# A linear-attention layer with one output-gate projection moved ahead of the second value projection, and a bias add and a division taken off VectorE

## The chip, the cores and the metric

One core of one Trainium2 chip runs the whole program. The metric is the device time of one execution in microseconds (us). Three runs of the kernel before gave a median of 1104.21 us (1104.09 to 1104.54).

## The reference, cut to what matters

Two blocks of two layers each work on 256 tokens of width 1024, in float32. The part that matters here is the linear-attention mixer of the second block: 4 heads with keys of width 128 and values of width 256, in chunks of 64 tokens.

```python
q, k, v, g, a_low = split(h @ w_in)
log_a = log_sigmoid(a_low @ w_gate_up + b_gate) / 16
bcum = cumsum(log_a within a chunk);  b_last = last of each chunk
q_in = q * 128 ** -0.5 * exp(bcum);  k_in = k * exp(-bcum);  k_dec = k * exp(b_last - bcum)
o = tril(q_in @ k_in.T) @ v + q_in @ S       # S: state carried over the chunks by k_dec and v
o = o * rsqrt(mean(o * o) + 1e-6) * head_norm_g * silu(g)
x = x + o @ w_out
```

## The kernel before, in words

**Weights.** A list made ahead (`plan_gla`, L1143) gives the order in which weights are loaded and used. Each piece of 128x4x512 float32 (1024 KB) comes by one DMA of SP's queue into one of 4 buffers `raw`, and serves two units of two 128-row blocks. ScalarE rounds a unit to `wh` (L294), VectorE takes the rest `wl = raw - wh` (L312); there are 5 buffers of each, and `unit` (L327) asks for the unit four ahead. Activations are kept as pairs too (`hh`, `hl`), and each product is three matmuls: `wh,hh`, `wl,hh`, `wh,hl` in the profile's names (`mm3`, L358; called a group below).

**Projections.** `proj` (L377) makes 128 tokens x 512 columns in each of two PSUM tiles `up` (3 buffers), for the token halves t = 0 and 1, in 16 groups. `proj_T` (L391) makes the transposed product, with 512 columns per matmul in two tiles; its result goes through `by_row` (L412, L416 and L419). `proj_wide` (L421) makes the first values and the 16 columns `a_low` together.

**Order.** The program is written out in Python. After every group `tick` (L202) advances a count and writes out whatever `after(n, f)` has put into a queue for that count; a consumer whose input isn't written out yet (`Act.wait`, L105) calls `force` (L215) until it is. `self.side` is a generator, `core`, that writes out a step of the attention between groups. A scheduler then puts each engine's instructions in a fixed order; of those whose inputs it takes to be ready, the one written out first goes first.

**The layer.** `gla` (L1151) uses its projections in this order: first values and `a_low` (`proj_wide`), second values (columns 1536), keys (512) and queries (0) by `proj_T`, the gate of heads 0 and 1 (2048), the gate of heads 2 and 3 (2560), then the output projection `accum` (L449) over y blocks 0 to 3 and 4 to 7.

- Five ticks after the first values, `gates` (L1185) turns `a_low` and `gates2` (L1190) makes the decay: a small matmul, the bias on VectorE (L1200, 4 times), `log_sigmoid` for two heads at a time (L900: Exp, Ln and Exp on ScalarE at L906, L910, L911, seven VectorE operations), the division by 16 (L1205, twice), a scan (L1208, 4 times), and the exponentials E, Ei, dec, Ed (L1210 to L1217). Keys and queries are multiplied by these (L1232, L1240).
- `core` (L1261) runs beside the gate projection of heads 0 and 1. Its step for heads 0 and 1 (j = 0) is written out after the 12th of the 16 groups, that of heads 2 and 3 (j = 1) after the 13th. Each makes o in PSUM, sums of squares (L1332, recorded at L556) and `hr` on GpSimd (L561, L563).
- `ev_g` (L1245) takes the gate out of PSUM with Silu (L1248), multiplies by the head gain (L1251, from `row`) and two ticks later calls `fin` (L1337): o times hr times gate (L1342, two per token half), then `prep` (L536): four transposes into the single buffer `tp` (L523), the rounding to `hh` on ScalarE (L509) and the rest `hl` on VectorE (L512). `accum` needs these pairs.

At the start of the program ScalarE is told to load one activation table that serves Exp and Ln (L1540).

Of the kernel before, what the change touches and what calls it, by code (L numbers as in the profile page):

```python
# [11 lines left out]
F32 = mybir.dt.float32  # L12
F32R = mybir.dt.float32r
I32 = mybir.dt.int32
AF = mybir.ActivationFunctionType
ALU = mybir.AluOpType
PSUM = bass.MemoryType.PSUM

P = 128
S = 256  # L20
# [140 lines left out]
class Builder:  # L161
# [981 lines left out]
    def plan_gla(self):  # L1143
        w = self.a["gla_w_in_2"][0]
        self.add_proj(self.a["gla_w_va"], 8, 0, WIDE)
        for c in (1536, 512, 0, 2048, 2560):
            self.add_proj(w, 8, c, 512)
        self.plan_rows(self.a["gla_w_out_2"][0], 0, 4)
        self.plan_rows(self.a["gla_w_out_2"][0], 4, 4)

    def gla(self, h, rs, hook):  # L1151
# [15 lines left out]
        def ev_v(i):  # L1167
            return lambda t, ps: self.scaled(v[t][:, i * 512:(i + 1) * 512], ps, rs[:, t:t + 1])
# [21 lines left out]
        def gates2():  # L1190
            bg = self.vec("bgate")
            z = [self.acc_tile() for _ in range(H)]
            for hd in range(H):
                rows = slice(32 * hd, 32 * hd + 16)
                self.nc.tensor.matmul(z[hd][:, 0:S], wg[rows, 0:P], aT[rows, :], start=True, stop=True,
                                      skip_group_check=True, tile_position=(32 * hd, 0))
            for j in range(2):
                zs = self.tmp_tile()
                for i in range(2):
                    nc.vector.tensor_scalar(out=zs[:, i * S:(i + 1) * S], in0=z[2 * j + i][:, 0:S],  # L1200
                                            scalar1=bg[:, 2 * j + i:2 * j + i + 1], scalar2=None, op0=ALU.add)
                e = [self.tmp_tile() for _ in range(4)]
                o = LA[:, j * 512:(j + 1) * 512]
                self.log_sigmoid(o, zs, e, 512)
                nc.vector.tensor_scalar(out=o, in0=o, scalar1=1.0 / 16.0, scalar2=None, op0=ALU.mult)  # L1205
                for i in range(2):
                    sl = slice((2 * j + i) * S, (2 * j + i + 1) * S)
                    nc.vector.tensor_tensor_scan(out=B[:, sl], data0=self.cst("reset"), data1=LA[:, sl], initial=0.0,  # L1208
                                                 op0=ALU.mult, op1=ALU.add)
            nc.scalar.activation(out=E, in_=B, func=AF.Exp)  # L1210
            nc.scalar.activation(out=Ei, in_=B, func=AF.Exp, scale=-1.0)
            b4 = B.rearrange("p (n c) -> p n c", c=64)
            bl = b4[:, :, 63:64]
            nc.scalar.activation(out=dec, in_=bl.rearrange("p n c -> p (n c)"), func=AF.Exp)
            nc.vector.tensor_tensor(out=Ed.rearrange("p (n c) -> p n c", c=64), in0=bl.to_broadcast([P, 16, 64]),
                                    in1=b4, op=ALU.subtract)
            nc.scalar.activation(out=Ed, in_=Ed, func=AF.Exp)  # L1217

        self.after(DLY[16], gates)
        self.proj(h, 8, 512, ev_v(1))  # L1220
        while self.q:
            self.force()
# [17 lines left out]
                nc.vector.tensor_tensor(out=half(E, b), in0=tk, in1=half(E, b), op=ALU.mult)  # L1240
            self.after(DLY[18], f)

        y = Act(self)

        def ev_g(i):  # L1245
            def f(t, ps):
                gs = self.tmp_tile()
                nc.scalar.activation(out=self.like(gs, ps), in_=ps, func=AF.Silu, scale=rs[:, t:t + 1])  # L1248

                def gain():  # L1250
                    nc.vector.tensor_tensor(out=gs, in0=gs, in1=hg[:, i * 512:(i + 1) * 512], op=ALU.mult)  # L1251
                    self.after(DLY[20], lambda: fin(t, i, gs))

                self.after(DLY[19], gain)
            return f

        oo = {}
        hs = self.small.tile([P, 8], F32, tag="hs", name="hs", bufs=1)
        hr = self.small.tile([P, 8], F32, tag="hr", name="hr", bufs=1)

        def core():  # L1261
            msk = self.gmask_i.unsqueeze(1).to_broadcast([P, H, P])
            kd = []
            both = self.att.tile([P, 2048], F32, tag="bias1", name="both")
            sc = [both[:, t * 1024:t * 1024 + 512] for t in range(2)]
            for s in sc:
                nc.gpsimd.memset(s, 0.0)
            yield 3
            for t in range(2):

                sp = self.up_tile()
                for hd in range(H):
                    for r in (0, 64):
                        sl = slice(hd * S + t * P + r, hd * S + t * P + r + 64)
                        self.mm(sp[r:r + 64, hd * 64:(hd + 1) * 64], Ei[:, sl], E[:, sl], True, True)
                for r in (0, 64):
                    nc.vector.copy_predicated(r4(sc[t])[r:r + 64, :, r:r + 64], msk[r:r + 64, :, r:r + 64],
                                              r4(sp[:, :256])[r:r + 64])
                yield 1
                tp = self.tp_tile()  # L1280
                for hd in range(H):
                    nc.tensor.transpose(tp[:, hd * P:(hd + 1) * P], Ed[:, hd * S + t * P:hd * S + t * P + P], self.ident)
                kk = both[:, t * 1024 + 512:(t + 1) * 1024]
                nc.scalar.copy(kk, tp)
                kd.append(kk)
                yield 1
            S01 = self.att.tile([P, 2048], F32, tag="bias0", name="S01")
            S2 = big("qT1")
            St = [S2 if n == 2 else S01[:, n * 1024:(n + 1) * 1024] for n in range(3)]

            def kv_tiles(j, ns):

                kv = [self.acc_tile() for _ in ns]
                for i in range(2):
                    hd = 2 * j + i
                    for m, n in enumerate(ns):
                        t, r = n // 2, 64 * (n % 2)
                        self.mm(kv[m][:, i * S:(i + 1) * S], kd[t][r:r + 64, hd * P:(hd + 1) * P],
                                v[t][r:r + 64, hd * S:(hd + 1) * S], True, True)
                return kv  # L1300

            def grow(j, n, kv):
                for i in range(2):
                    hd = 2 * j + i
                    sl = slice(hd * S, (hd + 1) * S)
                    nc.vector.scalar_tensor_tensor(out=St[n][:, sl], in0=St[n - 1][:, sl],
                                                   scalar=dec[:, hd * 4 + n:hd * 4 + n + 1],
                                                   in1=kv[:, i * S:(i + 1) * S], op0=ALU.mult, op1=ALU.add)

            for j in range(2):  # L1310
                kv = kv_tiles(j, (0, 1))
                nc.vector.tensor_copy(St[0][:, j * 512:(j + 1) * 512], kv[0])
                grow(j, 1, kv[1])
                yield 1
            for j in range(2):
                grow(j, 2, kv_tiles(j, (2,))[0])
                yield 1
            for j in range(2):
                o = [self.acc_tile() for _ in range(2)]
                heads = range(2 * j, 2 * j + 2)  # L1320
                for t in range(2):
                    for i, hd in enumerate(heads):
                        self.mm(o[t][:, i * S:(i + 1) * S], sc[t][:, hd * P:(hd + 1) * P], v[t][:, hd * S:(hd + 1) * S],
                                i == 0, False)

                for i, n in ((0, 1), (0, 2), (0, 3), (1, 2), (1, 1), (1, 3)):
                    t, r, hd = n // 2, 64 * (n % 2), heads[i]
                    self.mm(o[t][r:r + 64, i * S:(i + 1) * S], E[:, hd * S + n * 64:hd * S + n * 64 + 64],
                            St[n - 1][:, hd * S:(hd + 1) * S], False, True)
                for t in range(2):  # L1330
                    for i in range(2):
                        self.square_sum(hs[:, 4 * j + 2 * t + i:4 * j + 2 * t + i + 1], o[t][:, i * S:(i + 1) * S], S, 1.0 / 16.0)  # L1332
                    oo[t, j] = o[t]
                self.rsqrt(hr[:, 4 * j:4 * j + 4], hs[:, 4 * j:4 * j + 4])
                yield 1

        def fin(t, j, gs):  # L1337
            o = oo.pop((t, j))
            yy = self.tmp_tile()
            for i in range(2):  # L1340
                sl = slice(i * S, (i + 1) * S)
# [6 lines left out]
        while self.q:  # L1348
            self.force()
        self.side = core()  # L1350
        self.proj(h, 8, 512, ev_g(0))
        while self.side is not None:
            self.step()
        self.proj(h, 8, 512, ev_g(1))
        acc = self.new_acc()
        self.accum(acc, y, [0, 1, 2, 3], True, False)
        self.accum(acc, y, [4, 5, 6, 7], False, True, self.add_x(hook))
# [395 lines left out]
```

## Time and profile before

| | |
|---|---|
| median of 3 runs | 1104.21 us |
| the profiled execution's own time | 1104.49 us |
| its span, first to last instruction | 1102.7 us |
| mean granted TensorE clock | 0.997 |
| busy: PE / VectorE (DVE) / ScalarE (ACT) / GpSimd (POOL) | 1087.3 / 801.4 / 609.2 / 30.4 us |

An engine's idle time matters only where it ends up as a wait of the engine that bounds the span. Times in the rows are counted from the span's start; a row's second number is the time from the first start to the last end of the instructions that it merges. DVE and ACT rows overlap slightly at their ends, because the next instruction starts while the one before drains.

### The profile page before, as it was taken

Reading aid. Unit: us, or ns where it says so; the run is one execution under the profiler, and the core shown is the slowest. Engines: PE = TensorE matmul, PEld = TensorE weight load, DVE = VectorE, ACT = ScalarE, POOL = GpSimd, SP = SyncE. Lnnn points to the kernel's source line nnn. Section 1 sums busy time; section 2 is a strip of 40 time slices with the busy share of each in tenths; the row PEclk is TensorE's granted clock in tenths of the full one; section 3 lists DMA queues with packets and bytes.
Section 4 is the critical chain, followed back from the end, with each engine's and each line's share of the span. In section 5 each row is a group of like instructions: output and inputs, shape, how many; then the busy total and the mean of one; then the engine's idle time right before and its main releaser. Section 6 shows DMA issues by size and latency. Waiting matters only on the chain.

```text
span 1102.7 us, 19201 instructions
## 1 busy us (share of the span) xinstructions
PE 1087.3 (99%) x7769; PEld 1003.4 (91%) x7769; DVE 801.4 (73%) x1200; ACT 609.2 (55%) x927; POOL 30.4 (3%) x55
## 2 busy tenths in 40 slices
PE   9999999999999999999999999999999999999997
PEld 7987999999988999999897899999999999999996
DVE  6687756556687766555788578787787768987786
ACT  6466655445665555545664556555555446565563
POOL 1000000000000000000010000000000000000001
PEclk9999999999999999999999999999999999999998
DMA  9844466655563566665555354566665664657551
GB/s 335 298 165 145 162 195 206 210 193 173 142 207 128 172 192 204 206 200 192 194 180 183 108 178 155 179 197 217 201 220 193 197 204 153 189 194 224 188 166 74
DMA packets 137801, 207.30 MB, mean 188 GB/s; under 512 B 10528, under 2 KB 65008, under 8 KB 137712
## 3 DMA queue, kind: packets, MB, share of 16 engines
q1 hardware_dynamic: 136576, 203.89, 56.8%
q10 hardware_dynamic: 1136, 2.17, 0.5%
q8 instruction: 61, 1.00, 0.4%
q14 instruction: 28, 0.23, 0.1%
HBM read 204.97 MB, written 1.07 MB: 187 GB/s over the span
## 4 chain that ended last, share of the span: by engine, by line
PE 87%; DVE 7%; ACT 2%; DMA 1%; issue 1%; SPq 0%; ACTq 0%; DVEq 0%
PE up L339 52%; PE acc L339 33%; DVE wl L312 2%; DMA raw<-fox_w_in 1%; ACT wh L294 1%; PE acc L523 1%; PE tp L523 1%; ACT p L697 1%; DVE p L716 1%; DVE x L602 0%; DVE p L707 0%; PE tp L533 0%; DVE tmp L1365 0%; DVE pT L725 0%; DVE kT L1232 0%
## 5 line engine op out<-in xcount | busy, mean ns | idle before, releaser
L312 DVE TENSOR_TENSOR wl<-raw,wh 128x1024 fp32r<-128x1024 f32 (+2 forms) x373 | 452.3, 1219 | 223.4 <-ACT wh L294 222.4
L294 ACT CAST wh<-raw 128x1024 fp32r<-128x1024 f32 (+2 forms) x373 | 388.8, 1043 | 381.7 <-PE up L339 253.1
L339 PE MATMUL up<-hh,wh 128*128 128x256 f32 x1564 | 431.7, 276 | 0.0
L339 PE MATMUL up<-hh,wl 128*128 128x256 f32 x1564 | 430.1, 275 | 0.0
L339 PE MATMUL up<-hl,wh 128*128 128x256 f32 x1564 | 429.4, 275 | 0.0
L339 PEld LDWEIGHTS up<-hh,wh 128*128 128x128 f32 x1564 | 300.1, 192 | 2.9 <-issue 1.5
L339 PEld LDWEIGHTS up<-hh,wl 128*128 128x128 f32 x1564 | 300.1, 192 | 0.9
L339 PEld LDWEIGHTS up<-hl,wh 128*128 128x128 f32 x1564 | 299.8, 192 | 0.3 <-DVE hl L512 0.2
L339 PE MATMUL acc<-wh,hh 128*128 128x512 f32 (+1 forms) x606 | 227.4, 375 | 0.2 <-DVE mx L716 0.2
L339 PE MATMUL acc<-wh,hl 128*128 128x512 f32 (+1 forms) x606 | 225.1, 371 | 0.1
L339 PE MATMUL acc<-wl,hh 128*128 128x512 f32 (+1 forms) x606 | 224.8, 371 | 0.0
L339 PEld LDWEIGHTS acc<-wh,hl 128*128 128x128 f32 x606 | 114.5, 189 | 15.4 <-DVE hl L1374 0.5
L339 PEld LDWEIGHTS acc<-wh,hh 128*128 128x128 f32 x606 | 114.6, 189 | 15.0 <-DVE mx L716 0.6
L339 PEld LDWEIGHTS acc<-wl,hh 128*128 128x128 f32 x606 | 114.7, 189 | 13.4
L1365 DVE SCALAR_TENSOR_TENSOR tmp<-tmp,vecs,tmp 128x255 f32<-128x255 f32 x192 | 78.0, 479 | 15.2 <-ACT tmp L1363 15.2
L339 PE MATMUL up<-wh,hh 128*128 128x512 f32 (+4 forms) x142 | 52.2, 370 | 1.8 <-DVE tmp L419 1.8
L339 PE MATMUL up<-wl,hh 128*128 128x512 f32 (+4 forms) x142 | 49.9, 352 | 0.2 <-DVE wl L312 0.2
L339 PE MATMUL up<-wh,hl 128*128 128x512 f32 (+4 forms) x142 | 49.8, 353 | 0.1
L1363 ACT ACTIVATE tmp<-tmp,vecs 128x256 f32<-128x256 f32 x96 | 40.9, 496 | 0.0
L1373 ACT CAST hh<-tmp 128x512 fp32r<-128x512 f32 x58 | 34.1, 619 | 8.3 <-DVE tmp L1418 8.3
L1374 DVE TENSOR_TENSOR hl<-tmp,hh 128x512 fp32r<-128x512 f32 x58 | 38.3, 685 | 0.0
L339 PEld LDWEIGHTS up<-wh,hh 128*128 128x128 f32 x142 | 26.8, 189 | 8.1 <-issue 5.5
(205 smaller groups left out, 769.8 us busy)
## 6 DMA issues: line engine op xcount, KB each, us to landing
raw<-ffn_w_up SPq DMA_DIRECT2D x176, 256.0 KB, 4.2
raw<-ffn_w_up SPq DMA_DIRECT2D x32, 1024.0 KB, 5.3
raw<-ffn_w_down SPq DMA_DIRECT2D x32, 1024.0 KB, 5.0
raw<-ffn_w_down SPq DMA_DIRECT2D x44, 512.0 KB, 6.6
raw<-sc_w_in SPq DMA_DIRECT2D x12, 1024.0 KB, 5.3
raw<-fox_w_in SPq DMA_DIRECT2D x10, 1024.0 KB, 9.7
raw<-gla_w_in SPq DMA_DIRECT2D x10, 1024.0 KB, 5.0
raw<-fox_w_out SPq DMA_DIRECT2D x4, 1024.0 KB, 5.2
```

The source lines that it names most:

```text
L294: self.last_hi = nc.scalar.copy(hi[:, :kn, :w], self.raws[r][:, k:k + kn])
L312: self.last_wl = nc.vector.tensor_tensor(out=u.lo[:, :kn, :w], in0=self.raws[r][:, k:k + kn], in1=u.hi[:, :kn, :w].bitcast(F32), op=ALU.su ...
L339: self.nc.tensor.matmul(out, lhsT, rhs, start=start, stop=stop, skip_group_check=True)
L523: self.nc.tensor.transpose(tp[:, i * P:(i + 1) * P], src[:, i * P:(i + 1) * P], self.ident)
L697: self.nc.scalar.activation(out=p[:, o:o + n], in_=p[:, o:o + n], func=AF.Exp, scale=scale, bias=nm[:, j:j + 1], accum_out=sm[:, j:j + 1])
L716: self.nc.vector.tensor_tensor_reduce(out=p[:, o:o + n], in0=lgs[h][:, w], in1=bias(h)[:, w], scale=1.0, scalar=NEG, op0=ALU.add, op1=ALU. ...
L1363: nc.scalar.activation(out=out, in_=z, func=AF.Copy, scale=w[:, 2:3])
L1365: nc.vector.scalar_tensor_tensor(out=out[:, d:], in0=z[:, :S - d], scalar=w[:, 2 - d:3 - d], in1=out[:, d:], op0=ALU.mult, op1=ALU.add)
L1373: nc.scalar.copy(hi, src)
L1374: nc.vector.tensor_tensor(out=lo, in0=src, in1=hi.bitcast(F32), op=ALU.subtract)
```

## The change

- The plan and the calls put the gate projection of heads 0 and 1 (columns 2048) right behind the first values, ahead of the second values. `core` now runs beside the gate projection of heads 2 and 3, which the output projection follows at once.
- The finished gate of heads 0 and 1 waits in two buffers of another pool until `core` has made o; `core` calls `fin` for these heads 4 and 5 ticks after their o. For heads 2 and 3 it is still called two ticks after the gain.
- The bias moves to ScalarE (Identity with a bias read from PSUM). The division by 16 goes: the scan runs over undivided logarithms, and the four exponentials take 1/16 as their scale.

```diff
     def plan_gla(self):
-        for c in (1536, 512, 0, 2048, 2560):
+        for c in (2048, 1536, 512, 0, 2560):
             self.add_proj(w, 8, c, 512)
...
                 for i in range(2):
-                    nc.vector.tensor_scalar(out=zs[:, i * S:(i + 1) * S], in0=z[2 * j + i][:, 0:S],
-                                            scalar1=bg[:, 2 * j + i:2 * j + i + 1], scalar2=None, op0=ALU.add)
+                    nc.scalar.activation(out=zs[:, i * S:(i + 1) * S], in_=z[2 * j + i][:, 0:S], func=AF.Identity,
+                                         bias=bg[:, 2 * j + i:2 * j + i + 1])
...
                 self.log_sigmoid(o, zs, e, 512)
-                nc.vector.tensor_scalar(out=o, in0=o, scalar1=1.0 / 16.0, scalar2=None, op0=ALU.mult)
...
-            nc.scalar.activation(out=E, in_=B, func=AF.Exp)
-            nc.scalar.activation(out=Ei, in_=B, func=AF.Exp, scale=-1.0)
+            nc.scalar.activation(out=E, in_=B, func=AF.Exp, scale=1.0 / 16.0)
+            nc.scalar.activation(out=Ei, in_=B, func=AF.Exp, scale=-1.0 / 16.0)
...
         self.after(DLY[16], gates)
+        y = Act(self)
+        oo, gates_of = {}, {}
+
+        def ev_g(i):
+            def f(t, ps):
+                gs = self.tmp_tile() if i else self.att.tile([P, 768], F32, tag="pT", name=self.name("gs"), bufs=2)[:, :512]
+                nc.scalar.activation(out=self.like(gs, ps), in_=ps, func=AF.Silu, scale=rs[:, t:t + 1])
+
+                def gain():
+                    nc.vector.tensor_tensor(out=gs, in0=gs, in1=hg[:, i * 512:(i + 1) * 512], op=ALU.mult)
+                    gates_of[t, i] = gs
+                    if i:
+                        self.after(DLY[20], lambda: fin(t, i))
+
+                self.after(DLY[19], gain)
+            return f
+
+        self.proj(h, 8, 512, ev_g(0))
         self.proj(h, 8, 512, ev_v(1))
...
                 self.rsqrt(hr[:, 4 * j:4 * j + 4], hs[:, 4 * j:4 * j + 4])
+                if j == 0:
+                    for t in range(2):
+                        self.after(4 + t, lambda t=t: fin(t, 0))
                 yield 1
...
         self.side = core()
-        self.proj(h, 8, 512, ev_g(0))
+        self.proj(h, 8, 512, ev_g(1))
         while self.side is not None:
             self.step()
-        self.proj(h, 8, 512, ev_g(1))
         acc = self.new_acc()
         self.accum(acc, y, [0, 1, 2, 3], True, False)
```

## Rows read from the trace of the kernel before

**Rows 1.** The page: busy time of each engine over the whole span.
```profile
PE 1087.3 (99%) x7769; PEld 1003.4 (91%) x7769; DVE 801.4 (73%) x1200; ACT 609.2 (55%) x927; POOL 30.4 (3%) x55
```

**Rows 2.** Waits of PE over the whole span: total us, times, longest us.
```profile
PE up L339 <- DVE tmp L419: 1.8, 1, 1.8
```

**Rows 3.** The chain that ended last, 585 to 600 us: start, us, what.
```profile
589.85 2.27 DVE wl L312 x2
592.12 0.68 DVE tmp L419 x2
...
592.93 3.99 PE up L339 x28
```

**Rows 4.** Stretches: length, PE, PEld, DVE, ACT, POOL busy (instructions), clock, DMA.
```profile
558.00:593.00 35.00, 33.25 (x253) 30.99 (x253) 33.52 (x50) 22.31 (x31) 0.00 (x0) 1.00 0.55 180
580.00:593.00 13.00, 11.25 (x99) 10.85 (x97) 13.00 (x19) 7.87 (x9) 0.00 (x0) 1.00 0.54 191
```

**Rows 5.** VectorE's groups, 568 to 593 us: busy us, mean ns.
```profile
L312 DVE TENSOR_TENSOR wl<-raw,wh 128x1024 fp32r<-128x1024 f32 x9 | 10.9, 1220 | 0.3 <-ACT wh L294 0.3
...
L1200 DVE TENSOR_SCALAR tmp<-acc,vecs 128x256 f32<-128x256 f32 x2 | 1.0, 480 | 0.0
L1205 DVE TENSOR_SCALAR LB<-LB 128x512 f32<-128x512 f32 x2 | 0.8, 418 | 0.0
```

**Rows 6.** ScalarE in order of time, 557 to 588 us.
```profile
557.46 0.48 ACT L616 ACTIVATE v<-up,rs 128x264 f32<-128x264 f32 x1 [1.89 <-POOL rs L1132]
...
568.74 1.25 ACT L616 ACTIVATE v<-up,rs 128x512 f32<-128x512 f32 x2
...
573.96 0.63 ACT L906 ACTIVATE tmp<-tmp 128x512 f32<-128x512 f32 x1 [1.11 <-DVE tmp L905]
...
587.05 1.06 ACT L1217 ACTIVATE kT<-kT 128x1024 f32<-128x1024 f32 x1
```

**Rows 7.** DMA issues over the span: KB each, us to landing.
```profile
row<-gla_head_norm_g ACTq DMA_DIRECT2D x1, 512.0 KB, 5.4
```

**Rows 8.** PE in order of time around the last steps of the attention.
```profile
616.14 0.48 PE L339 MATMUL up<-wh,hh 128*128 128x512 f32 x1
...
618.19 0.38 PE L339 MATMUL up<-wh,hh 128*128 128x512 f32 x1
...
622.72 0.60 PE L523 MATMUL tp<-ident,tmp 128*128 128x128 f32 x4
...
629.43 0.38 PE L339 MATMUL acc<-wh,hh 128*128 128x512 f32 x1
```

**Rows 9.** GpSimd, the scaling of heads 0 and 1.
```profile
613.73 1.01 POOL L563 TENSOR_TENSOR hr<-hr,mhalf 128x4 f32<-128x4 f32 x1
```

**Rows 10.** ScalarE in order of time, 617 to 624 us.
```profile
617.38 1.28 ACT L1248 ACT_TABLE_LOAD   x1
618.68 0.69 ACT L1248 ACTIVATE tmp<-up,rs 128x512 f32<-128x512 f32 x1
...
619.62 0.69 ACT L1248 ACTIVATE tmp<-up,rs 128x512 f32<-128x512 f32 x1
620.19 2.06 ACT L294 CAST wh<-raw 128x1024 fp32r<-128x1024 f32 x2
623.36 0.58 ACT L509 CAST hh<-tp 128x512 fp32r<-128x512 f32 x1 [1.12 <-PE tp L523]
```

**Rows 11.** VectorE in order of time, 609 to 628 us.
```profile
619.40 0.69 DVE L1251 TENSOR_TENSOR tmp<-tmp,row 128x512 f32<-128x512 f32 x1 [8.88 <-ACT tmp L1248]
620.22 0.48 DVE L1342 SCALAR_TENSOR_TENSOR tmp<-acc,hr,tmp 128x256 f32<-128x256 f32 x1
...
626.79 0.69 DVE L512 TENSOR_TENSOR hl<-tp,hh 128x512 fp32r<-128x512 f32 x1 [0.30 <-ACT hh L509]
```

**Rows 12.** Half-microsecond stretches at the end of the span, columns as in rows 4.
```profile
1094.50:1095.00 0.50, 0.05 (x1) 0.00 (x0) 0.50 (x2) 0.00 (x0) 0.30 (x1) 1.00 0.00 0
...
1096.50:1097.00 0.50, 0.00 (x0) 0.00 (x0) 0.32 (x3) 0.50 (x3) 0.00 (x0) 0.53 0.00 0
```

More of the change, by code (lines that the diff above doesn't have):

```diff
@@ L1209, in gates2 @@
                                                  op0=ALU.mult, op1=ALU.add)
-            nc.scalar.activation(out=E, in_=B, func=AF.Exp)
-            nc.scalar.activation(out=Ei, in_=B, func=AF.Exp, scale=-1.0)
+            nc.scalar.activation(out=E, in_=B, func=AF.Exp, scale=1.0 / 16.0)
+            nc.scalar.activation(out=Ei, in_=B, func=AF.Exp, scale=-1.0 / 16.0)
             b4 = B.rearrange("p (n c) -> p n c", c=64)
             bl = b4[:, :, 63:64]
-            nc.scalar.activation(out=dec, in_=bl.rearrange("p n c -> p (n c)"), func=AF.Exp)
+            nc.scalar.activation(out=dec, in_=bl.rearrange("p n c -> p (n c)"), func=AF.Exp, scale=1.0 / 16.0)
             nc.vector.tensor_tensor(out=Ed.rearrange("p (n c) -> p n c", c=64), in0=bl.to_broadcast([P, 16, 64]),
                                     in1=b4, op=ALU.subtract)
-            nc.scalar.activation(out=Ed, in_=Ed, func=AF.Exp)
+            nc.scalar.activation(out=Ed, in_=Ed, func=AF.Exp, scale=1.0 / 16.0)
         self.after(DLY[16], gates)
+        y = Act(self)
[12 more added lines that the diff above has]
+        self.proj(h, 8, 512, ev_g(0))
         self.proj(h, 8, 512, ev_v(1))
@@ L1241, in ev_q @@
             self.after(DLY[18], f)
[L1243 to L1257, printed above, removed]
         hs = self.small.tile([P, 8], F32, tag="hs", name="hs", bufs=1)
@@ L1334, in core, with fin @@
                 self.rsqrt(hr[:, 4 * j:4 * j + 4], hs[:, 4 * j:4 * j + 4])
+                if j == 0:
+                    for t in range(2):
+                        self.after(4 + t, lambda t=t: fin(t, 0))
                 yield 1
-        def fin(t, j, gs):
-            o = oo.pop((t, j))
+        def fin(t, j):
+            o, gs = oo.pop((t, j)), gates_of.pop((t, j))
             yy = self.tmp_tile()
```

## The prediction, made before the changed kernel was run

> **What bounds the kernel now.** I read the page first: PE is busy for 1087.3 of 1102.7 us [rows 1], so a reordering that adds and removes no matmuls can only win or lose waits of PE, and all of them together are 15.4 us. Next come the waits of PE by releaser. One lies in this layer: 1.8 us, once, for VectorE's L419 [rows 2]. The chain that ended last tells why L419 is late: two `wl` of 2.27 us together run ahead of it, and the chain changes from VectorE to PE only at 592.93 [rows 3]. The wait sits between the query projection and the gate projection behind it: the latter's second PSUM tile is one of the query's, and L419 empties it. The windows then show that this is a backlog and no single late instruction: VectorE is busy 33.52 of the 35 us from 558 to 593, and 13.00 of the last 13.00, while ScalarE has 22.31 of 35 [rows 4]. So the change is aimed at the right engine, and **its prize is at most about 1.8 us**, 0.16% of the run.
>
> Then I looked at where the changed kernel will want data sooner than now. Now a whole gate projection stands between the end of the attention and the output projection: it starts at 618.19, the output projection at 629.43 [rows 8], and the last `hl` that the first four blocks need starts at 626.79 and takes 0.69 [rows 11], 1.9 us early. The change removes this 11 us cover, because its first gate projection has been spent ahead of the values.
>
> **VectorE's relief.** Four bias adds of 0.48 and two divisions of 0.42 leave VectorE [rows 5]: 2.8 us. With the gate projection, four `wl` of 1.22 [rows 5] and two gains (L1251) of 0.69 [rows 11] move into the stretch, 6.3 us, and PE's time for it grows by a projection, some 10.5 us (the 11.2 above less two sets of four transposes). So 33.5 - 2.8 + 6.3 = 37.0 us stand in about 45 where 33.5 stood in 35; the backlog goes, and with it the 1.8 us. What can be late next at that place is one `wl` ahead of L419, 1.2 us; I take nothing for it and keep 0 to 1.2 for the range.
>
> **ScalarE's load.** The bias on ScalarE isn't in the trace. Its nearest row is a scaled copy out of PSUM, 128x264 in 0.48 us [rows 6]; four are 1.9 us. Two Silu of 0.69 come ahead [rows 10]. They will run where the second values are now taken out, at 568.74, between the Exp, Ln and Exp of the first two heads and the next Exp at 573.96 [rows 6]. Silu loads its own table, 1.28 us [rows 10]; the set that serves Exp and Ln together was asked for by hand at L1540 and isn't asked for again. So between one table (a single load back) and three (Exp, Ln, Exp apart) come after it: with Silu's own, 2 to 4 added loads. I take 4, 5.1 us. With four more `wh` of 1.03 (half of the 2.06 for two) [rows 10] ScalarE gets 22.3 + 1.9 + 1.4 + 5.1 + 4.1 = 34.8 of 45 us. Three loads lie in the chain of the decay, which ends now with L1217 at 588.1 [rows 6]; less 2.8 and plus 3.8 it ends near 589, while the keys come out only when the key projection ends, about 10.5 us later than now. Cost on the path: nothing, hidden by the moved projection; without that cover it would be the 1.0 us. Silu also frees PSUM for the second values; their first tile is the third buffer, so groups of the other token half can go first. I keep 0 to 0.5 for this.
>
> Here a rule speaks against the change: "ScalarE: Activation LUTs" of the Trainium skill, in "What ACT_TABLE_LOAD costs", tells to expect about 2.66 us for each change of set, a drain of 1.38 behind the load included. This trace doesn't agree: the load takes 1.28 from 617.38 [rows 10], and Silu starts at 618.68, at once after its end. By the page four changes would be 10.6 us and the decay would end some 4 us later than I have it, still before the attention needs the queries, so the sum would be the same.
>
> **DMA and queues.** SP's queue issues the same pieces of the same size in another order of columns, each when its buffer comes free: no cost. The gain's row goes out on ScalarE's queue ahead of the first values and lands in 5.4 us [rows 7]; the moved gain comes a whole projection later.
>
> **The new wait.** Use the clock of before for the end of the attention, as its steps and the 16 groups beside it are the same. The o of heads 2 and 3 is done when the group at 616.14 begins; three groups of 0.68 end at 618.19 [rows 8]. GpSimd has `hr` for heads 0 and 1 by 614.74 [rows 9], and VectorE idles 8.9 us up to 619.40 [rows 11], so `fin` can run early. Its four transposes can't: they are written out after the last group of the projection, and PE has groups ready until 618.19. From there the path is transposes (0.60 [rows 8]), rounding (0.58 [rows 10]), rest (0.69 [rows 11]): 1.9 us, of which the transposes' 0.4 are work done today as well. That is the lower bound: 1.5 us of wait.
> But ScalarE isn't free. The table load of the second gate starts at 617.38, the Silu of its second token half ends at 620.31, and then a `wh` of 1.03 for the output weights is both ready (its buffer comes free at 618.19) and written out ahead of the rounding [rows 10]. So the rounding runs from about 621.2 to 621.8 and the rest to 622.6: a wait of 4.0 us behind the transposes. On VectorE two `fin` operations of 0.48 [rows 11] for heads 2 and 3 stand ahead of the rest too, which makes up to 5.0. I take 4.5, in the middle, since both are in front by the order of writing. The second token half follows through the single `tp` buffer, but four groups of the first half (2.7 us) cover its 1.9; blocks 4 to 7 have the whole first half of the output projection.
>
> **Sum.** 4.5 - 1.8 = 2.7 us on the profiled execution's own 1104.49 (span 1102.7 and 1.8 around it), or 1107.2. The median of the runs is 0.3 lower than that execution, so I predict **1106.9 us**. About 0.2%, or 2.2 us, is what a measurement of this kernel can tell from no change.
>
> **Rivals.**
> - *In time (0.28).* The transposes get between the last groups, or the rounding gets ahead of Silu and `wh`, so the new wait is 0 to 1.5 us and the 1.8 is won: 1102.4 to 1103.9, not slower. For it: o, `hr` and the gate are all there by 614.74, 3.4 us before the projection ends, and the scheduler does move instructions: half of `fin` (620.22) comes ahead of the second gain, written out earlier [rows 11]. Against it: PE would have to pass over ready groups. It decides at a new wait under 1.8 us.
> - *The clock falls (0.22).* An idle PE can lose its clock: the last matmul ends by 1094.6 and the granted clock reads 1.00 until 1096.5, then 0.5, the lower of the two levels [rows 12]. So 2 us of idleness sufficed there, and 1.8 at 592 did not (clock 1.00 [rows 4]). If a 4.5 us wait does it, each group after it costs 0.68 more until the clock is back. No row shows a return; between nothing and four groups (2.7 us) I take three: 1109.
> - *Nothing is won (0.08).* Table loads and Silu delay the decay or `wl`, and L419 is late as now: 1104.2 + 4.5 = 1108.7. Against it: 8 us of slack on VectorE.
>
> "TensorE: Matmul & The Clock Gate" of the Trainium skill, in "Why this matters for your kernels", likewise warns of idle PE gaps in mid-kernel; the end of this trace agrees.
>
> **How the numbers follow.** The forecast has 0.42; of its 4.0 to 5.0 less 1.8, with up to 0.5 unwon, a quarter stays within 2.2 us. Slower by over 0.2%: 0.32 + 0.21 + 0.06 = 0.59. Within: 0.10 + 0.22 + 0.02 = 0.34. Faster by over 0.2% needs the whole prize and something that I don't see: 0.07. The range runs from the full prize, 1102.4, to the clock's rival with its upper end, 1109.6; alone, the forecast's range is 1106 to 1108.
>
> **What would show it.** Right: no PE wait on L419; a PE wait of 4 to 5 us at the first matmul of the output projection, released by `hl` L512, with Silu and `wh` just ahead of L509 on ScalarE; five table loads in this layer instead of one. Wrong: transposes of heads 0 and 1 between the last groups of the gate projection, and no new PE wait over 1.8 us.

## The result, and the profile after

The changed kernel takes **1110.7 us** (median of 4 runs, 1110.23 to 1111.28), beside 1104.38 (1104.09 to 1104.57) for the kernel before on the same chip: a ratio of 1.0058 [1.0046, 1.0070] (in brackets, here and below, the 95% interval), slower by 6.3 us. Forecast were 1106.9 and, as range, 1102.4 to 1109.6: the sign was right, the loss more than twice the 2.7 forecast, and the time lies above the range. The profiled execution took 1110.23 with a span of 1108.5; before it was 1104.49 and 1102.7.

The page, busy time of each engine, after [rows 1]:

```profile
PE 1090.8 (98%) x7769; PEld 1005.9 (91%) x7769; DVE 799.6 (72%) x1194; ACT 615.5 (56%) x935; POOL 30.4 (3%) x55
```

VectorE has six instructions fewer. ScalarE has eight more, the four biases and four table loads. PE has the same 7769 matmuls but is busy 3.5 us longer: a first sign that some of them ran at a lower clock.

Waits of PE from 585 to 645 us, after: total us, times, longest us [rows 2]:

```profile
PE tp L523 <- DVE tmp L1349: 2.2, 1, 2.2
PE tp L523 <- DVE hl L512: 1.4, 1, 1.4
PE acc L339 <- ACT hh L509: 0.7, 1, 0.7
```

The wait on L419 is gone, which was the prize. In its place stand three new ones, all between the last group of the gate projection of heads 2 and 3 and the second group of the output projection. PE in order of time there [rows 8]:

```profile
626.39 0.38 PE L339 MATMUL up<-wl,hh 128*128 128x512 f32 x1
626.60 0.38 PE L339 MATMUL up<-wh,hl 128*128 128x512 f32 x1
629.17 0.83 PE L523 MATMUL tp<-ident,tmp 128*128 128x128 f32 x4 [2.19 <-DVE tmp L1349]
630.68 0.62 PE L339 MATMUL acc<-wh,hh 128*128 128x512 f32 x1 [0.68 <-ACT hh L509]
...
633.11 1.11 PE L523 MATMUL tp<-ident,tmp 128*128 128x128 f32 x4 [1.38 <-DVE hl L512]
...
634.44 0.63 PE L339 MATMUL acc<-wh,hh 128*128 128x512 f32 x1
634.87 0.64 PE L339 MATMUL acc<-wl,hh 128*128 128x512 f32 x1
```

Compare the distance from start to start: 0.21 us in the first two rows, 0.43 us (634.44 to 634.87) in the last two, for a matmul of the same size. The clock has halved. Windows over this stretch, after (columns as in [rows 4]; the clock is the third number from the end):

```profile
628.00:630.00 2.00, 0.83 (x4) 0.41 (x4) 1.97 (x5) 1.87 (x4) 1.33 (x2) 1.00 0.00 0
630.00:632.00 2.00, 1.05 (x3) 0.33 (x2) 2.00 (x6) 0.59 (x1) 0.00 (x0) 0.72 0.00 0
632.00:634.00 2.00, 0.89 (x5) 0.90 (x5) 2.00 (x4) 0.00 (x0) 0.00 (x0) 0.50 0.00 0
...
636.00:638.00 2.00, 2.00 (x8) 1.61 (x8) 0.00 (x0) 0.01 (x1) 0.00 (x0) 0.57 0.00 0
638.00:640.00 2.00, 2.00 (x12) 1.59 (x11) 0.76 (x2) 1.63 (x2) 0.00 (x0) 1.00 0.00 0
```

From about 630.9 to 637.7 the granted clock is 0.5, that is 1.2 instead of 2.4 GHz, long after PE has work again at 633.11. What holds PE up before that is on VectorE, in order of time [rows 11]:

```profile
628.03 0.69 DVE L1230 TENSOR_TENSOR tmp<-tmp,row 128x512 f32<-128x512 f32 x1 [8.88 <-ACT tmp L1227]
628.63 1.65 DVE L1349 SCALAR_TENSOR_TENSOR tmp<-acc,hr,gs 128x256 f32<-128x256 f32 x4
630.21 0.68 DVE L1230 TENSOR_TENSOR tmp<-tmp,row 128x512 f32<-128x512 f32 x1
630.80 1.65 DVE L1349 SCALAR_TENSOR_TENSOR tmp<-acc,hr,tmp 128x256 f32<-128x256 f32 x4
632.37 0.68 DVE L512 TENSOR_TENSOR hl<-tp,hh 128x512 fp32r<-128x512 f32 x1
```

VectorE stands idle for 8.88 us and then does in one run what PE waits for. The `fin` of heads 0 and 1 (L1349 with `gs`) has had its inputs since 623.4, when GpSimd's `hr` was done, but in VectorE's fixed order it stands behind the gain (L1230) of heads 2 and 3, and that waits for Silu. ScalarE in order of time [rows 10]:

```profile
626.01 1.28 ACT L1227 ACT_TABLE_LOAD   x1
627.31 0.69 ACT L1227 ACTIVATE tmp<-up,rs 128x512 f32<-128x512 f32 x1
...
628.25 0.69 ACT L1227 ACTIVATE tmp<-up,rs 128x512 f32<-128x512 f32 x1
628.82 1.05 ACT L294 CAST wh<-raw 128x1024 fp32r<-128x1024 f32 x1
630.04 0.59 ACT L509 CAST hh<-tp 128x512 fp32r<-128x512 f32 x1 [0.17 <-PE tp L523]
```

**Where the time went.** Two starts on PE serve as anchors: the last matmul of the last gate projection (before 629.21, after 626.60), and the first matmul of the next layer, `up<-hh,wh` (before 652.01, after 658.00). Before:

```profile
629.21 0.38 PE L339 MATMUL up<-wh,hl 128*128 128x512 f32 x1
...
652.01 0.27 PE L339 MATMUL up<-hh,wh 128*128 128x256 f32 x1
```

After, the second one (the first stands above):

```profile
658.00 0.27 PE L339 MATMUL up<-hh,wh 128*128 128x256 f32 x1
```

Up to the first anchor the changed kernel is 2.6 us ahead: 1.8 of L419, and two sets of transposes (0.36 each, 0.72) that it has still to do; the rest is 0.1. Between the anchors it takes 31.40 instead of 22.80 us, 8.6 more, of which 0.72 are those transposes. That leaves 7.9 us for the wait and the clock together; the experiments divide them.

### The profile page after: what moved, and what is told of

It is laid out like the page before. It is cut to its first block, busy times and chain, and to the rows that moved or that the text cites. A ratio compares the mean times of both kernels' runs of the same rounds, so it can differ in the third digit from the quotient of the medians.

```text
span 1108.5 us, 19201 instructions
## 1 busy us (share of the span) xinstructions
PE 1090.8 (98%) x7769; PEld 1005.9 (91%) x7769; DVE 799.6 (72%) x1194; ACT 615.5 (56%) x935; POOL 30.4 (3%) x55
## 3 DMA queue, kind: packets, MB, share of 16 engines
q10 hardware_dynamic: 1136, 2.17, 0.6%
## 4 chain that ended last, share of the span: by engine, by line
PE 88%; DVE 6%; ACT 3%; DMA 1%; issue 1%; SPq 0%; ACTq 0%; DVEq 0%
PE up L339 52%; PE acc L339 34%; DVE wl L312 2%; DMA raw<-fox_w_in 1%; ACT wh L294 1%; PE acc L523 1%; PE tp L523 1%; ACT p L697 1%; DVE p L716 1%; DVE x L602 0%; DVE p L707 0%; PE tp L533 0%; SPq L264 0%; DVE tmp L1371 0%; ACT junk L556 0%
```

## The experiments

Two theories at the start. *The move*: the cover that the gate projection gave to the end of the attention is gone, and all of the loss stands between the two anchors. *Its rival*: table loads, biases on ScalarE or the other order of weights cost something elsewhere. Within the move, the wait's length was claimed by VectorE's order, by ScalarE's queue and by the clock.

**e1: only the relief of VectorE, in the kernel before.**

```diff
-                    nc.vector.tensor_scalar(out=zs[:, i * S:(i + 1) * S], in0=z[2 * j + i][:, 0:S],
-                                            scalar1=bg[:, 2 * j + i:2 * j + i + 1], scalar2=None, op0=ALU.add)
+                    nc.scalar.activation(out=zs[:, i * S:(i + 1) * S], in_=z[2 * j + i][:, 0:S], func=AF.Identity,
+                                         bias=bg[:, 2 * j + i:2 * j + i + 1])
...
-                nc.vector.tensor_scalar(out=o, in0=o, scalar1=1.0 / 16.0, scalar2=None, op0=ALU.mult)
...
-            nc.scalar.activation(out=E, in_=B, func=AF.Exp)
+            nc.scalar.activation(out=E, in_=B, func=AF.Exp, scale=1.0 / 16.0)
```

(and so for the other three exponentials)

> The kernel before with the bias on ScalarE and without the division, all projections in the old order. If the wait of 1.8 us on L419 is VectorE's backlog, 2.8 us less work removes it: no PE wait on L419 and 1102.6 us. If the projection had to move for that, the wait stays and the time is 1104.4.

Measured: 1102.65 us (1102.17 to 1103.00), ratio 0.9985 [0.9976, 0.9994]: 1.6 us faster than before. All that is left of the wait of 1.8 [rows 2] is this (waits of PE, 560 to 640 us):

```profile
PE up L339 <- DVE tmp L419: 0.3, 1, 0.3
```

The anchors stand at 627.84 and 650.64, 22.80 apart as before: everything gained is gained ahead of the first.

**e3 and e8: the division alone, the bias alone.** e3 has the hunks of e1 on the division and the exponentials, e8 the one on the bias.

> The kernel before with the division alone taken away (scales of 1/16 in the exponentials). VectorE loses 0.84 us: if the wait is its backlog, about half of it goes, 1103.3 to 1103.7. If only the order counts, 1104.3.

> The kernel before with the bias alone on ScalarE. VectorE loses 1.9 us of work, a little more than the wait on L419: if its backlog is the whole wait, 1102.6 to 1102.9. If the wait comes from the order of two wl ahead of L419 and not from the backlog, 1104.3.

Measured: 1103.75 (0.9994 [0.9985, 1.0003]) without the division, with 1.2 us left of the wait on L419; 1103.36 (0.9992 [0.9983, 1.0001]) with the bias on ScalarE, with 1.0 left. So 0.84 us of division took 0.6 off the wait, 1.92 us of bias 0.8, and both together, 2.76 us, took 1.5: a microsecond taken off VectorE is worth 0.4 to 0.7 here. The first two biases bring nothing: without them VectorE waits 0.96 us for the same biases on ScalarE (e1 and e8, at L904). The other two take 0.39 each from start to start in VectorE's row before (570.02 to 570.41) and the divisions 0.33 each, together 1.4 us, near the 1.5. Each time by itself is inside what this measurement can tell; but their gains, 0.6 and 1.0, add up to the 1.6 of e1. Both expectations missed a little: e3 lies just above its 1103.3 to 1103.7, and e8 lies between its two values, since it had counted all four biases in full.

**e2: the moved projection without the relief.** The changed kernel with bias and division back on VectorE (the diff of e1, reversed).

> The changed kernel with bias and division put back on VectorE: the moved projection alone. If the loss is all in the new wait behind the last gate projection, and the move itself has slack enough for VectorE, the time is that of the changed kernel, 1110 to 1111, with no wait on L419. If the relief is what removes that wait, it comes back and the time is 1112 to 1113.

Measured: 1111.23 (1110.72 to 1112.16), 1.0066 [1.0052, 1.0079]. Waits of PE, 585 to 645 us:

```profile
PE tp L523 <- DVE tmp L1350: 2.2, 1, 2.2
PE tp L523 <- DVE hl L512: 1.2, 1, 1.2
PE acc L339 <- ACT hh L509: 0.7, 1, 0.7
PE up L339 <- DVE tmp L419: 0.5, 1, 0.5
```

The time lies between the two that were expected. The same three waits and nearly the whole loss come from the move alone; the clock is at 0.50 from 632 to 638 here too. The move by itself takes the wait on L419 from 1.8 to 0.5, and the relief beside it is worth at most the last 0.5 (the ratios of the two kernels overlap). So each half of the change does most of what the other does for L419, and only one of them has a price.

**e4: `fin` of heads 0 and 1 written out earlier.** It is called 1 and 2 ticks after o instead of 4 and 5.

```diff
-                        self.after(4 + t, lambda t=t: fin(t, 0))
+                        self.after(1 + t, lambda t=t: fin(t, 0))
```

> The changed kernel with fin of heads 0 and 1 written out 1 and 2 ticks after their o instead of 4 and 5, its transposes still written out after the projection. If VectorE's fixed order (fin behind the second gate's gain) sets the new wait, the transposes start at once when the projection ends, the wait falls by 2 us or more, the clock stays up and the time is under 1107. If the rounding and the rest behind Silu and the other heads' fin set it, about 1 us is saved and the clock still falls: 1109 to 1110.

Measured: 1110.28 (1109.51 to 1110.99), 1.0053 [1.0040, 1.0065]; only 0.4 under the changed kernel, within the scatter of both, and a little over the 1109 to 1110 expected for this case. VectorE and PE, in order of time:

```profile
623.67 1.66 DVE L1349 SCALAR_TENSOR_TENSOR tmp<-acc,hr,gs 128x256 f32<-128x256 f32 x4 [4.27 <-POOL hr L563]
...
630.16 0.48 DVE L1349 SCALAR_TENSOR_TENSOR tmp<-acc,hr,tmp 128x256 f32<-128x256 f32 x1 [1.18 <-POOL hr L563]
...
631.16 1.26 DVE L1349 SCALAR_TENSOR_TENSOR tmp<-acc,hr,tmp 128x256 f32<-128x256 f32 x3
632.34 0.68 DVE L512 TENSOR_TENSOR hl<-tp,hh 128x512 fp32r<-128x512 f32 x1
```

```profile
627.08 0.60 PE L523 MATMUL tp<-ident,tmp 128*128 128x128 f32 x4
630.67 0.48 PE L339 MATMUL acc<-wh,hh 128*128 128x512 f32 x1 [3.00 <-ACT hh L509]
...
633.07 1.11 PE L523 MATMUL tp<-ident,tmp 128*128 128x128 f32 x4 [1.70 <-DVE hl L512]
```

`fin` is done by 625.3 and the transposes stand right behind the last group, 2.1 us earlier than after, and `hl` still starts at 632.34 (after: 632.37). The first wait has only moved to the next stations: `hh` waits on ScalarE for Silu and a `wh` (629.08 to 630.02), and `hl` on VectorE for the `fin` operations of heads 2 and 3. This is the path on which the prediction counted the wait, with one part that it did not have: the first of those operations waits 1.18 us for GpSimd's `hr` of heads 2 and 3, and the last sum of squares for that runs on ScalarE behind Silu (628.16). What this wait costs by itself no run shows.

The clock falls here too, but later. It is still at 1.00 behind the wait of 3.0 us (window), falls at about 632.7, in the second wait, and is back at 636.1: 3.4 us at half clock, where the changed kernel has 6.8.

```profile
630.00:632.00 2.00, 0.70 (x2) 0.30 (x2) 1.84 (x5) 0.62 (x2) 0.13 (x1) 1.00 0.00 0
```

**e5: e4, with the transposes of heads 0 and 1 written out together with their `fin`.**

```diff
-            self.after(DLY[21], lambda: self.prep(yy, t, list(range(4 * j, 4 * j + 4)), [(y, None)]))
+            self.after(DLY[21] if j else 0, lambda: self.prep(yy, t, list(range(4 * j, 4 * j + 4)), [(y, None)]))
```

> As the run before it, and the transposes of heads 0 and 1 are written out with no delay, so that they stand between the last groups of the gate projection. If the missing cover is the whole loss, no PE wait over 0.5 us is left at the output projection, the clock stays at its upper level, and only the win on L419 remains: 1102.4 to 1103.5. If something else in the new order costs time (table loads, the bias on ScalarE), it stays above 1105.

Measured: 1103.71 (1103.50 to 1104.83), 0.9997 [0.9988, 1.0005], 0.2 over the range expected. PE in order of time:

```profile
623.96 0.83 PE L523 MATMUL tp<-ident,tmp 128*128 128x128 f32 x4 [0.40 <-DVE tmp L1349]
...
627.35 0.60 PE L523 MATMUL tp<-ident,tmp 128*128 128x128 f32 x4
...
628.43 0.38 PE L339 MATMUL up<-wh,hl 128*128 128x512 f32 x1
628.65 0.38 PE L339 MATMUL acc<-wh,hh 128*128 128x512 f32 x1
```

The output projection follows the gate projection 0.22 us later, with no wait; the anchors are 22.93 apart (before 22.80). Two delays in the order of writing, this and e4's, take back 7.0 us. So the loss isn't in the other order of weights, nor in table loads: it is that the last steps of heads 0 and 1 were written out where nothing was left to lie under. Yet e5 is 1.06 us above e1 (its profile has PE waits of 0.4 for `fin` and 0.2 for Silu's tile, where e1 has only the 0.3 on L419), so even without its loss the move has nothing to offer that the relief hasn't given.

**e6: the changed kernel with PE kept busy through the first wait.** It adds work whose result isn't read.

```diff
+        wm = self.up_tile()
+        for i in range(16):
+            nc.tensor.transpose(wm[:, (i % 4) * P:(i % 4 + 1) * P], self.ident, self.ident)
         acc = self.new_acc()
```

> The changed kernel with 16 more transposes of the identity on PE (into a free PSUM tile that nobody reads) between the last group of the gate projection and the transposes of heads 0 and 1. They fill most of the first 2.2 us of the wait and computed nothing is used. If the fallen clock costs 2.5 to 3 us by itself, the clock now stays at its upper level and the time falls to 1107.5 to 1108.5, although PE has more to do. If the wait alone is the loss, the time stays at 1110.7 or rises.

Measured: 1109.77, but from 1108.43 to 1111.05, 1.0050 [1.0037, 1.0062]: the median missed what was expected. The profiled execution, one of the shorter at 1108.7, had the clock at 1.00 in all windows of this stretch, among them this one:

```profile
632.00:634.00 2.00, 0.27 (x2) 0.27 (x3) 2.00 (x5) 0.00 (x0) 0.00 (x0) 1.00 0.00 0
```

Its `hl` starts 5.77 us after the first anchor (633.00 and 627.23), exactly as after (632.37 and 626.60), and its anchors are 29.26 apart instead of 31.40. With the same wait, the clock is thus worth 2.1 us in this execution. Whether the clock fell nevertheless in the longer executions is not shown: there is no trace of one, and their mean granted clock, 0.997 beside 0.998 in the two shortest, differs no more than it does among executions of the kernel before (0.997 to 0.999).

**e7: e4, with the rounding of heads 0 and 1 ahead of `wh`, and `fin` of heads 2 and 3 four ticks later.**

```diff
-                        self.after(DLY[20], lambda: fin(t, i))
+                        self.after(DLY[20] + 4, lambda: fin(t, i))
...
+        y.wait(0, 0)
         acc = self.new_acc()
```

> As the run with fin written out early, and further: the rounding and rest of the first token half are written out ahead of the next weights, and fin of heads 2 and 3 four ticks later. If the queues of ScalarE and VectorE set the length of the wait, the rest (hl) comes about 1.2 us earlier (two fin operations and one wh less ahead of it) and the time falls by 1 to 2 us, to 1108.5 to 1109.3. If the transposes behind the last group set it, nothing changes: 1110.3.

Measured: 1109.05 (1108.64 to 1109.77), 1.0044 [1.0031, 1.0058], with waits of 2.0 for `hh` and 1.0 for `hl` where e4 has 3.0 and 1.7. The queues of ScalarE and VectorE do set the wait's length, but the clock still falls, at about 629.4, right behind the first wait of 2.0 us (windows):

```profile
628.00:630.00 2.00, 0.71 (x2) 0.44 (x2) 0.82 (x2) 2.00 (x5) 1.33 (x2) 0.85 0.00 0
630.00:632.00 2.00, 0.99 (x5) 0.54 (x4) 2.00 (x5) 0.18 (x1) 0.00 (x0) 0.50 0.00 0
...
636.00:638.00 2.00, 2.00 (x10) 1.70 (x10) 0.07 (x1) 1.05 (x1) 0.00 (x0) 0.95 0.00 0
```

**e9: e7, with the 16 transposes of e6 inside the wait for `hh`.**

```diff
         y.wait(0, 0)
+        wm = self.up_tile()
+        for i in range(16):
+            nc.tensor.transpose(wm[:, (i % 4) * P:(i % 4 + 1) * P], self.ident, self.ident)
```

> The kernel of e7 (transposes of heads 0 and 1 right behind the gate projection, the rounding ahead of the weight cast), with 16 transposes of the identity into a free PSUM tile that nothing reads, written behind those transposes, so that PE works through most of the 2.0 us wait for the rounding. They wait for nothing and last about as long as that wait (16 of them took 1.9 us in e6). If the granted clock costs what the theory says, it stays at 1.00 here in the profiled execution and in all others, and the time is 2.5 to 3 us under e7's 1109.05: 1106.0 to 1106.8. If the clock's fall is only a label on time that is lost anyway to the queues of ScalarE and VectorE, the time is e7's, 1108.7 to 1109.4. If the transposes are put ahead of the real ones, everything comes 2 us later: over 1109.4. A scatter as in e6 (2.6 us between executions) would mean that the clock still falls in some of them.

Measured: 1106.9 (nine of eleven runs from 1106.41 to 1107.14, two at 1108.39 and 1108.49), 1.0026 [1.0017, 1.0035]: 2.15 us under e7, a little less than was expected. PE in order of time, and its window where e7 has 0.50:

```profile
626.94 0.60 PE L523 MATMUL tp<-ident,tmp 128*128 128x128 f32 x4
627.37 1.91 PE L1364 MATMUL up<-ident 128*128 128x128 f32 x16
629.58 0.48 PE L339 MATMUL acc<-wh,hh 128*128 128x512 f32 x1 [0.30 <-ACT hh L509]
...
631.75 0.66 PE L523 MATMUL tp<-ident,tmp 128*128 128x128 f32 x4 [1.47 <-DVE hl L512]
```

```profile
630.00:632.00 2.00, 0.53 (x4) 0.25 (x3) 1.99 (x4) 0.47 (x1) 0.00 (x0) 1.00 0.00 0
```

This kernel does 1.9 us of work that nothing needs, in a wait in which PE couldn't do anything else, and is faster for it. Its anchors are 27.84 apart, those of e7 30.01: 2.17 us. Two pairs, after with e6 and e7 with e9, give the same **2.1 to 2.2 us for the clock**, both with 6.8 us at half clock in the execution without the added transposes. The medians differ by 0.9 in the first pair and by 2.15 in the second. What makes the two long executions of e9 long is not shown; e5, which has no such wait, also has two that are about 1 us longer than its others.

## Why the prediction was right in sign and too small

- **L419: right.** The wait went in full. 1.8 was the prize of the change, and the relief alone wins 1.6 of it (e1), as the backlog on VectorE had it.
- **Hidden work: right.** Four loads of 1.28 and four biases (mean 464 ns, taken as 480) were added on ScalarE, and PE has no wait in their stretch (e2, e4, e5 and e7 have one of 0.2 to 0.3 for Silu's tile, inside the 0 to 0.5 kept for it). The decay's last exponential (L1217) starts at 587.68, where [rows 6] have 587.05; the forecast end near 589 came at 588.7.
- **"So `fin` can run early": false.** VectorE was idle, but its order had been fixed with the gain of heads 2 and 3 in front. It was read as an engine that takes what is ready. It cost little: e4 repairs it and wins 0.4, since the path through Silu, `wh`, GpSimd's `hr` and the other `fin` ends at the same time.
- **The new wait: mechanism right, size too small.** Between the anchors 31.40 less 22.80, less 0.72 of transposes, less 2.14 of clock (e6) leaves 5.7 us, where 4.5 was taken from bounds of 4.0 and 5.0. It was to show as one wait of 4 to 5 us at the first matmul, released by `hl`; it came as three waits of 4.3 us in all, and only one of them is put down to `hl`. (5.7 is more than 4.3 because the profile counts a matmul as busy for 0.38 us, while in a gapless row the next one starts after 0.21: each break costs more than the wait shown.) ScalarE's part came as worked out: in e4 the rounding starts 2.6 us after the point where the transposes end at full clock (627.44 to 630.02), as 618.6 to 621.2 had it. VectorE's part was mis-sized: the term had up to two operations of 0.48 ahead of the rest, 1.0 us; in e4 the rounding ends at 630.6 and VectorE still has the end of a gain and three of those operations to do, until 632.4, because the first of the four could only start at 630.16, behind GpSimd's `hr`; the term had nothing for that wait of 1.18 us. So `hl` ends at 633.02, 5.6 us behind that point instead of the upper bound of 5.0. In the changed kernel itself two gains and eight `fin` operations run in one row from 628.03 on and end at the same time.
- **The clock: the step that failed.** The forecast left it at full, and gave its fall to a rival with 0.22, though the forecast's own wait of 4.5 us was well over the 2 us of idleness that the end of the span had shown to suffice [rows 12]. The runs show the clock at 0.5 for 6.8 us and 2.1 us lost to it (after and e6). The price was near, 2.0 taken from three groups, in part by luck: three was chosen between none and four, and in e4's profiled execution the clock was down for only half as long. With the rival's 1109 the error would have been 1.7 us instead of 3.8.
- **The sum, put right:** 5.7 + 2.1 − 1.8 = 6.0 us. Of the 3.3 us that the forecast's 2.7 lacks, the clock is 2.1 and the wait 1.2. The profiled spans differ by 5.8, the medians by 6.3; the profiled execution of the changed kernel is one of its two shorter ones.
- **Rivals.** *In time* didn't come about as written; e5 shows that it was two delays in the order of writing away: transposes between the last groups, no wait, no loss. *Nothing is won* fell with the wait on L419. *The clock falls* came true. The warning of the Trainium skill against idle PE gaps in mid-kernel ("TensorE: Matmul & The Clock Gate", "Why this matters for your kernels") is borne out by the 0.50 in the windows, in e7 already behind a wait of 2.0 us.

The version to keep is e1: the relief without the move, 1.6 us faster than the kernel before and 8 us faster than the changed one.

## What to carry to other kernels

Before work is moved away, look at what it covered and write the covered steps earlier too: here two delays in the order of writing decided 7.0 us (1110.7 to 1103.7). An engine's idle time in a profile doesn't say that it will take a new ready instruction; look at what stands ahead of it in that engine's order. And where a forecast wait on PE is longer than a stretch of idleness after which the same trace shows the clock falling, the cost of a fallen clock belongs into the sum and not only into a rival, with a range: here the clock fell behind a wait of 2.0 us in e7, and behind one of 3.0 in e4 it had not fallen yet.

## What the runs showed of the hardware that wasn't expected

- The clock fell though PE wasn't idle all the time: after, PE's last group ended at 626.98, 0.83 us of transposes followed at 629.17, and at about 630.9 the clock went to half. Half-microsecond windows:

```profile
630.50:631.00 0.50, 0.32 (x1) 0.32 (x2) 0.50 (x2) 0.12 (x1) 0.00 (x0) 0.89 0.00 0
...
637.50:638.00 0.50, 0.50 (x4) 0.49 (x3) 0.00 (x0) 0.01 (x1) 0.00 (x0) 0.78 0.00 0
```

  It came back at about 637.7, 4.6 us after PE had gapless work again at 633.11; in e4 it came back after 3.1 us of such work (633.07 to 636.1). At half clock, 512 columns take 0.43 us from start to start, at full clock 0.21 to 0.22; "TensorE: Matmul & The Clock Gate" of the Trainium skill, in "Wait — 56ns, not 53.3ns?", has 426.7 and 215.7 ns, and the rows agree.
- Transposes of the identity, whose result nothing reads, kept the clock at 1.00 in both profiled executions that have them (e6, e9), where their partners without them fell to 0.50. Whether they do so in each execution no run shows.
- Three loads came for one logarithm: after Silu's table, the lines of Exp, Ln and Exp each got their own. ScalarE in order of time, after:

```profile
571.94 1.28 ACT L906 ACT_TABLE_LOAD   x1
...
575.76 1.28 ACT L910 ACT_TABLE_LOAD   x1
...
578.64 1.28 ACT L911 ACT_TABLE_LOAD   x1
```

  "ScalarE: Activation LUTs" of the Trainium skill, in "Table sets: the hidden batching unit", names a set that holds both functions, so that one load would do. The rows differ: behind Silu, where no line of the kernel asks for that set again, Exp, Ln and Exp each brought a load of their own, 3.85 us for the three instead of 1.28. Ahead of Silu, with the set that was asked for at the start of the program, the same three run without a load (564.92 to 567.99).
